# Rotary embedding on one core: the cosine and sine rows loaded into partitions 0 to 62 instead of 0 to 124

## The chip, the core and the metric

The kernel runs on one core of one Trainium2 chip. The metric is the time of one execution on the device in microseconds (us). A second source is a profiled execution, whose trace gives the start and end of every instruction, the landing of every DMA, and a record (start, duration, bytes) of every DMA packet. The "span" is the time in that trace from the first to the last instruction.

## The reference

`x` is 16 batches x 512 positions x 1024 columns of float32, that is 16 heads of 64. `cos` and `sin` are 512 x 32, one row for each position.

```
x1, x2 = x[..., :32], x[..., 32:]          # halves of each head
out = concatenate([x1 * cos - x2 * sin,
                   x1 * sin + x2 * cos], axis=-1)
```

33.6 MB of `x` go in, as much comes out, and each table is 64 KB.

## The kernel before

**Tiling.** `x` is cut into 8 slabs of 2 batches. Two slabs make a pair, and a pair lies in one SBUF tile of 128 partitions x 16,384 float32. Partition p of a pair holds 16 successive positions, 16(p mod 32) to 16(p mod 32)+15. The first 8 positions of every partition are the even slab, the other 8 the odd one. So the tables are needed in 32 different pieces of 16 positions (`TP` = 32), and each piece in four partitions: p, p+32, p+64, p+96. There are three places for pairs; the fourth pair (slabs 6 and 7) takes the first place again.

**The tables.** A piece is 16 positions x 32 numbers = 512 float32 = 2 KB. One DMA for each table (line 87) puts the 32 pieces into every fourth partition, 0, 4 ... 124 (`TS` = 4, line 35), of a tile that VectorE has cleared (line 86), so the other partitions hold zeros. VectorE casts both tables to bf16 (line 107). GpSimd builds the selection matrix `pick` (lines 97 and 100): for column j of each group of 32 columns it sets the row p with p - TS*j = 0 to 1 (and, in a second copy, to -1). TensorE multiplies (line 114): output partition p gets the table row of piece p mod 32, so every partition has its own cosines and sines, in two PSUM tiles, one for even and one for odd slabs. VectorE copies the first to a bf16 table `tab` (line 121), ScalarE the second (line 155).

**A slab's work.** ScalarE casts the float32 slab to bf16 in place (line 155); VectorE multiplies it by the two tables (line 171, two instructions) and adds the crossed halves (line 174); ScalarE casts back to float32 (line 155), and the pair is stored.

**Order of the DMAs.** All DMAs are issued by SyncE (line 66) in one queue, in program order: slab 0 (128 rows of 32 KB), the cosine table, the sine table, slab 1 (128 rows of 32 KB), then the two pairs of slabs 2 to 5, each as two DMAs of 64 rows of 64 KB (even partitions, odd partitions). Later come the stores of slabs 0-1, the loads of slabs 6-7 into the place that those stores leave, and the other three stores, each when ScalarE is done with its pair.

Of the kernel before, what the change touches and what calls it, by code (L numbers as in the profile page):

```python
# [2 lines left out]

# [4 lines left out]


@with_exitstack  # L10
def kernel(
    ctx: ExitStack,
    tc: tile.TileContext,
    x: bass.AP,
    cos: bass.AP,
    sin: bass.AP,
    num_heads: int,
    out: bass.AP,
):
    nc = tc.nc  # L20
    P = nc.NUM_PARTITIONS

    batch, seq, dim = x.shape
    nh = num_heads
    hd = dim // nh
    half = hd // 2
    bf16 = mybir.dt.bfloat16
    f32 = mybir.dt.float32

    nb = 2  # L30
    nslabs = batch // nb
    rpp = nb * seq // P
    W = rpp * dim
    TP = seq // (2 * rpp)
    TS = P // TP
    TW = 2 * rpp * half

    out_flat = out.rearrange("b s h d -> b s (h d)")

    singles = ctx.enter_context(tc.tile_pool(name="singles", bufs=1))  # L40
    pairs = ctx.enter_context(tc.tile_pool(name="pairs", bufs=3))
    psum = ctx.enter_context(tc.tile_pool(
        name="psum", bufs=1, space=bass.MemoryType.PSUM))


    def view(t, offset, *dims):
        return dataclasses.replace(t, offset=t.offset + offset,
                                   ap=[t.ap[0], *[list(d) for d in dims]])

    places = [pairs.tile([P, 2 * W], f32, tag="pair", name="pair") for _ in range(3)]


    def here(s, n=1):
        return view(places[s // 2 % 3], s % 2 * W, (1, n * W))


    def there(t, s, n=1):  # L60
        return bass.AP(tensor=t.tensor, offset=t.offset + s // 2 * 2 * P * W + s % 2 * W,
                       ap=[[2 * W, P], [1, n * W]])


    def issue(out, in_):
        tc.keep_in_program_order(nc.sync.dma_start(out=out, in_=in_))  # L66


    def load(s, n=1, parts=slice(None)):
        issue(here(s, n)[parts], there(x, s, n)[parts])  # L70


    def store(s, n=1, parts=slice(None)):
        issue(there(out_flat, s, n)[parts], here(s, n)[parts])


    EVEN, ODD = slice(0, P, 2), slice(1, P, 2)


    load(0)  # L80


    cos_sb = singles.tile([P, TW], f32, tag="cos_sb")
    sin_sb = singles.tile([P, TW], f32, tag="sin_sb")
    for t, src in ((cos_sb, cos), (sin_sb, sin)):
        nc.vector.memset(t, 0.0)  # L86
        issue(t[::TS], bass.AP(
            tensor=src.tensor, offset=src.offset, ap=[[TW, TP], [1, TW]]))

    load(1)  # L90
    for s in (2, 4):
        for parts in (EVEN, ODD):
            load(s, 2, parts)


    pick = singles.tile([P, 2 * P], bf16, tag="pick")
    nc.gpsimd.memset(pick, 0.0)  # L97
    for g in range(2):
        part = view(pick, g * P, (TP, P // TP), (1, TP))
        nc.gpsimd.affine_select(  # L100
            out=part, in_=part, compare_op=mybir.AluOpType.not_equal,
            fill=1.0 - 2.0 * g, base=0, pattern=[[0, P // TP], [-TS, TP]],
            channel_multiplier=1)

    tab1 = singles.tile([P, 2 * TW], bf16, tag="tab1")
    for i, t in enumerate((cos_sb, sin_sb)):
        nc.vector.tensor_copy(out=view(tab1, i * TW, (1, TW)), in_=t)  # L107

    accs, tabs = [], []
    for h in range(2):  # L110
        acc = psum.tile([P, 2 * rpp * hd], f32, tag=f"acc{h}", name="acc")
        for i in range(2):
            for f in range(2):
                nc.tensor.matmul(  # L114
                    view(acc, i * rpp * hd + f * half, (hd, rpp), (1, half)),
                    view(pick, i * f * P, (1, P)),
                    view(tab1, i * TW + h * rpp * half, (half, rpp), (1, half)),
                    start=True, stop=True)
        accs.append(acc)
        tabs.append(singles.tile([P, 2 * rpp * hd], bf16, tag=f"tab{h}", name="tab"))  # L120
    nc.vector.tensor_copy(out=tabs[0], in_=accs[0])  # L121

    PART = 3 * dim
    LAST = {1: dim, 3: dim // 2}
    passes = []
    for s in range(nslabs):
        r = 0  # L130
        for n in {0: (4, 4), nslabs - 1: (4, 2, 2)}.get(s, (rpp,)):
            passes.append((s, r, n))
            r += n


    def halves(u):
        s, r, n = u
        t = here(s).bitcast(bf16)
        return [view(t, (2 * r + i * n) * dim, (1, n * dim)) for i in range(2)]


    def cast(u, a=0, b=None):
        s, r, n = u
        m = (n * dim if b is None else b) - a
        copy(view(halves(u)[0], a, (1, m)), view(here(s), r * dim + a, (1, m)))


    def copy_out(u, a=0, b=None):
        s, r, n = u
        m = (n * dim if b is None else b) - a  # L150
        copy(view(here(s), r * dim + a, (1, m)), view(halves(u)[1], a, (1, m)))


    def copy(out, in_):
        tc.keep_in_program_order(nc.scalar.copy(out=out, in_=in_))  # L155


    for i, u in enumerate(passes):
        s, r, n = u
        if i == 0:  # L160
            cast(u)
            cast(passes[1])
            copy(tabs[1], accs[1])
            cast(passes[2])
        elif s > 0 and not r:
            for v in passes:
                if v[0] == s + 1:
                    cast(v, PART if v[0] == 3 else 0)
        lo, up = halves(u)
        for t, a in ((up, 0), (lo, rpp * hd)):  # L170
            nc.vector.tensor_mul(  # L171
                out=t, in0=lo,
                in1=view(tabs[s % 2], a + r * hd, (hd, n), (0, nh), (1, hd)))
        nc.vector.tensor_add(  # L174
            out=up, in0=up, in1=view(lo, half, (hd, n * nh), (-half, 2), (1, half)))

        if s == 1:
            copy_out(u, 0, n * dim - LAST[s])
            cast((3, 0, rpp), 0, PART)
            copy_out(u, n * dim - LAST[s])  # L180
            for act in (store, load):
                for parts in (EVEN, ODD):
                    act(0 if act is store else 6, 2, parts)
        elif s == 3:
            copy_out(u, 0, n * dim - LAST[s])
        else:
            copy_out(u)
        if s == 4:
            copy_out((3, 0, rpp), rpp * dim - LAST[3])
            store(2, 2)  # L190
        elif s > 4 and s % 2 and r + n == rpp:
            for parts in (EVEN, ODD) if s == 5 else (slice(None),):
                store(s - 1, 2, parts)


# [1 line left out]
_INS = ['x', 'cos', 'sin', 'num_heads']  # L197
_OUTS = [((16, 512, 16, 64), 'float32')]

_NUMBERS = {'num_heads': 16}  # L200


# [26 lines left out]
```

## Time and profile before

| | |
|---|---|
| time, median of 3 runs (lowest to highest) | 161.15 us (160.95 to 161.81) |
| time of the profiled execution | 161.17 us |
| its span | 159.4 us (1.77 us lie around it) |
| ScalarE (ACT) busy | 114.3 us, 72% of the span |
| VectorE (DVE) busy | 109.6 us, 69% |
| TensorE (PE) busy | 1.9 us in 8 matmuls |
| DMA | 67.24 MB, mean 422 GB/s over the span |
| granted TensorE clock | 1.0 |

How to read it: the busy shares are of the whole span. The DMA packets' time is given as a share of 16 DMA engines' span: at 100% all sixteen would move data from the first instruction to the last. "SPq" is the queue of SyncE, from which every DMA here is issued; a DMA's line shows the issue, and its landing is a time of its own. Where a line ends in "<-", the name behind the arrow is what ended the wait.

### The profile page before, as it was taken

The numbers are of one execution on the slowest core, as the hardware profiler recorded it, in microseconds if no ns is written. First come the engines' busy times: TensorE is split into PE (matmuls) and PEld (weight loads), VectorE is DVE, ScalarE is ACT, GpSimd is POOL, SyncE is SP. The second block draws the span as 40 slices with busy tenths as digits, with TensorE's granted clock in tenths as the row PEclk, the third lists the DMA queues.
The fourth block names the chain that finished last, engine by engine and source line by source line (L and its number), as shares of the span: only waits on it lengthen the run. The fifth ranks groups of instructions, "written<-read, shape, count | busy, mean of one in ns | idle before, by whom it ended". The sixth has DMA issues, their size and how long they took to land.

```text
span 159.4 us, 178 instructions
## 1 busy us (share of the span) xinstructions
PE 1.9 (1%) x8; PEld 1.1 (1%) x8; DVE 109.6 (69%) x38; ACT 114.3 (72%) x27; POOL 1.1 (1%) x7
## 2 busy tenths in 40 slices
PE   0004000000000000000000000000000000000000
PEld 0002000000000000000000000000000000000000
DVE  2004899999806998999899999909999997000000
ACT  3007949992399999999999996799999969400000
POOL 2000000000000000000000000000000000000000
DMA  7999999899799699699698996996996996996993
GB/s 263 395 395 444 493 411 526 378 411 526 313 477 526 280 510 526 263 526 526 263 526 362 428 526 263 526 526 263 526 510 280 526 510 280 526 493 296 526 395 132
DMA packets 1472, 67.24 MB, mean 422 GB/s; under 512 B 256, under 2 KB 256, under 8 KB 320
## 3 DMA queue, kind: packets, MB, share of 16 engines
q1 hardware_dynamic: 1472, 67.24, 98.0%
HBM read 33.69 MB, written 33.55 MB: 422 GB/s over the span
## 4 chain that ended last, share of the span: by engine, by line
DMA 50%; DVE 15%; ACT 13%; issue 6%; ACTq 2%; SPq 1%
DMA pair<-in_x_dram 36%; DMA out_dram<-pair 14%; ACT pair L155 13%; DVE pair L171 10%; DVE pair L174 4%; ACTq L224 2%; SPq L66 1%; DVE sin_sb L86 0%; DVE cos_sb L86 0%; ACTq L155 0%
## 5 line engine op out<-in xcount | busy, mean ns | idle before, releaser
L155 ACT CAST pair<-pair 128x8192 bf16<-128x8192 f32 (+11 forms) x25 | 112.2, 4557 | 22.2 <-DMA pair<-in_x_dram 20.7
L171 DVE TENSOR_TENSOR pair<-pair,tab 128x8192 bf16<-128x8192 bf16 (+2 forms) x22 | 71.4, 3259 | 11.8 <-ACT pair L155 11.4
L174 DVE TENSOR_TENSOR pair<-pair 128x8192 bf16<-128x8192 bf16 (+2 forms) x11 | 35.8, 3259 | 0.3
L107 DVE CAST tab<-cos_sb 128x512 bf16<-128x512 f32 x1 | 0.4, 427 | 11.1 <-DMA cos_sb<-in_cos_dram 11.1
L114 PE MATMUL acc<-tab,pick 128*128 128x256 bf16 x8 | 1.9, 415 | 13.6 <-DVE tab L107 13.6
L121 DVE CAST tab<-acc 128x1024 bf16<-128x1024 f32 x1 | 1.2, 1225 | 1.0 <-PE acc L114 1.0
L155 ACT ACT_TABLE_LOAD x1 | 1.3, 1283 | 0.7 <-PEq L210 0.7
L114 PEld LDWEIGHTS <-pick 128*128 128x128 bf16 x8 | 1.1, 139 | 13.8 <-issue 12.0
L86 DVE MEMSET cos_sb<- 128x512 f32 x1 | 0.5, 485 | 0.9 <-PEq L210 0.9
L155 ACT CAST tab<-acc 128x1024 bf16<-128x1024 f32 x1 | 1.0, 1003 | 0.0
L100 POOL TENSOR_SCALAR_AFFINE_SELECT pick<-pick 128x128 bf16<-128x128 bf16 x2 | 0.6, 308 | 0.1
L86 DVE MEMSET sin_sb<- 128x512 f32 x1 | 0.5, 485 | 0.1
L107 DVE CAST tab<-sin_sb 128x512 bf16<-128x512 f32 x1 | 0.4, 421 | 0.0
L97 POOL MEMSET pick<- 128x256 bf16 x1 | 0.3, 311 | 0.3 <-POOLq L210 0.3
L210 POOL MEMSET const-bfloat16-1.0<- 128x1 bf16 x1 | 0.1, 101 | 0.0
L210 POOL MEMSET const-uint8-127<- 128x1 uint8 x1 | 0.1, 101 | 0.0
L210 POOL MEMSET const-float32-0.0<- 128x1 f32 x1 | 0.1, 98 | 0.2 <-issue 0.2
L210 POOL MEMSET const-float32-1.0<- 128x1 f32 x1 | 0.1, 98 | 0.0
## 6 DMA issues: line engine op xcount, KB each, us to landing
pair<-in_x_dram SPq DMA_DIRECT2D x2, 4096.0 KB, 16.1
pair<-in_x_dram SPq DMA_DIRECT2D x6, 33.8
out_dram<-pair SPq DMA_DIRECT2D x6, 21.5
cos_sb<-in_cos_dram SPq DMA_DIRECT2D x1, 64.0 KB, 11.6
sin_sb<-in_sin_dram SPq DMA_DIRECT2D x1, 64.0 KB, 11.1
```

Source lines behind the costliest of these rows:

```text
L66: tc.keep_in_program_order(nc.sync.dma_start(out=out, in_=in_))
L86: nc.vector.memset(t, 0.0)
L97: nc.gpsimd.memset(pick, 0.0)
L100: nc.gpsimd.affine_select(out=part, in_=part, compare_op=mybir.AluOpType.not_equal, fill=1.0 - 2.0 * g, base=0, pattern=[[0, P // TP], [-T ...
L107: nc.vector.tensor_copy(out=view(tab1, i * TW, (1, TW)), in_=t)
L114: nc.tensor.matmul(view(acc, i * rpp * hd + f * half, (hd, rpp), (1, half)), view(pick, i * f * P, (1, P)), view(tab1, i * TW + h * rpp * ...
L121: nc.vector.tensor_copy(out=tabs[0], in_=accs[0])
L155: tc.keep_in_program_order(nc.scalar.copy(out=out, in_=in_))
L171: nc.vector.tensor_mul(out=t, in0=lo, in1=view(tabs[s % 2], a + r * hd, (hd, n), (0, nh), (1, hd)))
L174: nc.vector.tensor_add(out=up, in0=up, in1=view(lo, half, (hd, n * nh), (-half, 2), (1, half)))
L210: nc = _bacc.Bacc("TRN2", target_bir_lowering=False, num_devices=1)
L224: with _tile.TileContext(nc) as tc:
```

## The change

The stride between the table pieces becomes 2 instead of 4, so the 32 pieces go to partitions 0, 2 ... 62. The slice of the destination gets an end, since partitions 64 to 126 are not written any more by these DMAs. The selection matrix follows through `TS` in the pattern of line 102 (row 2j instead of row 4j for column j). The instructions of every engine, their order, their sizes and their waits are the same in both kernels.

```diff
     TP = seq // (2 * rpp)
-    TS = P // TP
+    TS = P // TP // 2
     TW = 2 * rpp * half
...
     for t, src in ((cos_sb, cos), (sin_sb, sin)):
         nc.vector.memset(t, 0.0)
-        issue(t[::TS], bass.AP(
+        issue(t[:TP * TS:TS], bass.AP(
             tensor=src.tensor, offset=src.offset, ap=[[TW, TP], [1, TW]]))
```

## The prediction

> **What bounds the kernel now.** I read the engines' busy shares first, then the row of the DMA queue, then the slices of the span.
>
> ```profile
> PE 1.9 (1%) x8; PEld 1.1 (1%) x8; DVE 109.6 (69%) x38; ACT 114.3 (72%) x27; POOL 1.1 (1%) x7
> ...
> DMA  7999999899799699699698996996996996996993
> ...
> q1 hardware_dynamic: 1472, 67.24, 98.0%
> ```
>
> No compute engine is busy over 72%. The packets of the one DMA queue take 98.0% of sixteen engines' 159.4 us, that is 156.2 us on each engine. The digits of the slices swing between 6 and 9 because packets are long against a slice; the total says that no engine ever rests for long. The trace's packet records give the parts: 896 packets of 64 KB (2418 ns each for nearly all), 256 of 32 KB (1213 ns for most, the first sixteen up to 2045), and 64 of 2 KB, which are the two tables, 84 ns each without exception. The first packet starts at 1.73 us and the last ends at 158.23, a window of 156.5 us: about 0.3 us of it is unused on a mean engine. So the DMA engines are the bound from end to end, and whatever adds time to an engine's chain of packets comes out at the end of the kernel.
>
> Next I looked at who waits for the tables, in the timeline of the first stage and the waits.
>
> ```profile
> 12.81 7.11 ACT L155 CAST pair<-pair 128x4096 bf16<-128x4096 f32 x2 [10.81 <-DMA pair<-in_x_dram]
> 13.08 0.43 DVE L107 CAST tab<-cos_sb 128x512 bf16<-128x512 f32 x1 [11.14 <-DMA cos_sb<-in_cos_dram]
> 13.42 0.42 DVE L107 CAST tab<-sin_sb 128x512 bf16<-128x512 f32 x1
> 13.56 1.87 PE L114 MATMUL acc<-tab,pick 128*128 128x256 bf16 x8 [13.56 <-DVE tab L107]
> 13.56 1.38 PEld L114 LDWEIGHTS <-pick 128*128 128x128 bf16 x7 [11.99 <-issue]
> 14.82 1.23 DVE L121 CAST tab<-acc 128x1024 bf16<-128x1024 f32 x1 [0.98 <-PE acc L114]
> 16.45 6.82 DVE L171 TENSOR_TENSOR pair<-pair,tab 128x4096 bf16<-128x4096 bf16 x3 [0.41 <-ACT pair L155]
> ```
>
> ```profile
> ACT pair L155 <- DMA pair<-in_x_dram: 20.7, 4, 10.8
> ...
> DVE pair L171 <- ACT pair L155: 11.4, 5, 6.0
> ```
>
> The reader is to see that the tables land right behind slab 0 (the first cast starts at 12.81, the cosine cast at 13.08), and that the path from them (cast, matmul, copy to `tab`) ends at 14.82 + 1.23 = 16.05. VectorE's first multiply comes 0.4 us later, and what it waited for was ScalarE's cast. So the tables have 0.41 us to spare. Behind that lies more: ScalarE waits for a later load up to 42.25 us (5.38 us idle before it in the timeline), and VectorE waits for ScalarE for 6.0 us up to 49.30. A late table of up to 0.41 + 5.4 = 5.8 us is taken up before any store is late.
>
> **The change part by part.**
>
> Instructions: the order of each engine is the same in both kernels, with the same shapes and waits. VectorE's two clears (485 ns each) and two casts (427 and 421 ns) work on 128 partitions either way; GpSimd's two selections (308 ns) only take another step; the 8 matmuls (415 ns) still sum over 128 partitions, most of them zero. SyncE's two issues (567 and 577 ns) still have 32 rows of 2 KB. All this is 0 us, and it all lies before 16.45 us, beside loads that go on until 61 us.
>
> DMA: what is left is where the 64 packets of 2 KB go, in the stretch from 11.9 to 12.8 us. Today they are spread evenly: the sixteen completions of slab 0 come from 12.318 to 12.794 us, those of cosine from 12.524 to 12.982, those of sine from 12.709 to 13.155, each some 0.2 us behind the DMA ahead. That is two packets of 84 ns and a completion record of 9 ns, so each engine carries 2 + 2 table packets, 4 x 84 = 0.34 us of its 156.2.
>
> The trace has no DMA that writes only the lower 64 partitions: slabs 0 and 1 write all 128, and the loads by halves write every second partition from end to end. So the price is bounded from both sides. Lower end: the engines take rows by their number in the list, whatever the partition, and nothing is shared between engines on the way into SBUF: still 4 packets each, +0 us. Upper end by the even loads: the table work falls on half of the path, be it that an engine serves a fixed set of partitions (then 8 engines carry 8 packets each, 0.67 us, and 8 carry none), or that several engines meet at one entrance of SBUF (then 16 engines share 8 entrances, and each entrance passes twice the table bytes). Either way the slower half ends 8 x 84 - 4 x 84 = 336 ns later, **+0.34 us**. Below nothing: the sixteen engines do not end together (the last store's completions come from 157.97 to 158.56, 0.59 us apart). Were the eight that lose their table packets the late ones, the end could come up to 0.34 us sooner, -0.34 us.
>
> I take the upper end, +0.34. The rows nearest to it are the large packets. Sixteen engines move 64 KB each at the same time, and all but a few of 896 packets take the same 2418 ns, for DMAs of all partitions, of the even ones and of the odd ones, in and out. Were engines handed rows without regard to the partition, two of them would now and then meet at a place and one packet would be longer; such regularity fits a fixed share of the partitions for each engine. It fits a path without any sharing as well, which is the rival.
>
> [...]
>
> A delay of the tables by 0.34 us moves the end of the table path to 16.39, still ahead of 16.45, so VectorE does not wait. Slab 1 follows the tables in the queue and lands 0.34 us later on the slow engines, and from there every landing, every cast that waits for one, and the last store shift with it. The last store is issued at 137.28 while the DMA ahead of it lands from 138.66 on, so 1.38 us lie between; both ends shift alike, and no new gap opens.
>
> Sum against the profiled execution: 161.17 + 0.34 = 161.51 us. That execution is 0.02 above the median of 161.15, so no correction is made. A measurement of this kernel can tell about 0.5%, 0.8 us, from no change; the forecast is no difference that can be told.
>
> **The rivals.**
>
> The rows do not care about partitions: +0, 161.2 us. For it: 84 ns in every table packet, although they end beside 32 KB packets of other engines. Against it: the large packets' regularity. Chance 0.33.
>
> Balance: the engines that are relieved are the late ones, and the end comes 0.34 us sooner, 160.8 us. For it: a spread of 0.59 us at the end. Against it: the late ones would have to be all in one half of the engines. Chance 0.06.
>
> The other side, crowding on few engines: the 32 rows of step 2 go to so few engines that the tables clog their chains. All 64 packets are 64 x 84 = 5.38 us. On n engines the slowest chain grows by 5.38/n - 0.34. That exceeds 0.8 us only for n of 4 or less: 4 engines give +1.0, 162.2 us; 2 give +2.35, 163.5; one gives +5.0, 166.2. For it: the step and the span of the list are new to this kernel. Against it: DMAs of 128, 64 and 32 rows are all spread over sixteen completions now. A late table adds nothing even then, as 5.0 is under the 5.8 us of cover. Chance 0.10.
>
> That the change does not do what it says (engine and SBUF side unchanged) is the first rival.
>
> **How the numbers follow.** +0.34: 0.45; +0: 0.33; -0.34: 0.06; crowding: 0.10; a drift of the chip between the runs (the three runs of before lie 0.86 us apart) that moves a median by over 0.5%: 0.03 up and 0.03 down. Faster by over 0.5%: 0.03. Slower: 0.10 + 0.03 = 0.13. Within: 0.84. The range from 160.8 to 162.0 holds the first three cases (0.84) with 0.5 us for the runs' spread on top of the likeliest; crowding lies outside.
>
> **What would show it.** In the changed kernel's packet records the 64 table packets of 84 ns should be 8 on each of half the engines, or longer than 84 ns. The completions of the cosine DMA should trail those of slab 0 by 0.34 us on the slow engines instead of 0.2, and slab 1's last landing (22.82) should come at about 23.2. VectorE's first multiply stays at about 16.45 with a wait on ScalarE. The share of the DMA queue stays at 98%. If the sine cast starts over 1 us later than 13.42, the rows are crowded on few engines. If the time moves by over 0.8 us while the first 23 us of the trace stay as they are, my account is wrong at its root, for then something later in the kernel depends on these partitions.

## The result and the profile after

The changed kernel takes 163.26 us (median of 6 runs, 163.04 to 164.26) beside 161.28 us for the kernel before (6 runs): the ratio is 1.0134, 95% interval 1.0101 to 1.0167. It is slower by about 2 us, where the forecast was 0.34 us and no difference that can be told. The profiled execution took 163.04 us with a span of 161.2 us. (The ratios in this document leave disturbed runs out and are not the quotients of the medians.)

The first view is taken from the page of the changed kernel: busy shares, slices, and the DMA queue.

```profile
PE 1.9 (1%) x8; PEld 1.1 (1%) x8; DVE 109.7 (68%) x38; ACT 114.3 (71%) x27; POOL 1.1 (1%) x7
...
DMA  7999999979979979979799899899899899896990
...
q1 hardware_dynamic: 1472, 67.24, 97.5%
```

The compute engines do the same work in the same time. The DMA engines still move the same 67.24 MB in 1472 packets, and their packets take 97.5% of a longer span: 0.975 x 161.2 = 157.2 us on a mean engine, against 156.2 before. So the mean engine is busy for 1.0 us more with the same bytes, and idle for about 0.9 us more (the span grew by 1.86 us).

The next view is the timeline of the first stage after the change.

```profile
13.11 7.11 ACT L155 CAST pair<-pair 128x4096 bf16<-128x4096 f32 x2 [11.11 <-DMA pair<-in_x_dram]
13.54 0.43 DVE L107 CAST tab<-cos_sb 128x512 bf16<-128x512 f32 x1 [11.61 <-DMA cos_sb<-in_cos_dram]
13.90 0.43 DVE L107 CAST tab<-sin_sb 128x512 bf16<-128x512 f32 x1
...
15.29 1.23 DVE L121 CAST tab<-acc 128x1024 bf16<-128x1024 f32 x1 [0.96 <-PE acc L114]
16.75 6.82 DVE L171 TENSOR_TENSOR pair<-pair,tab 128x4096 bf16<-128x4096 bf16 x3 [0.24 <-ACT pair L155]
```

Slab 0 is cast 0.30 us later, the tables 0.46 us later, and the first multiply still waits for ScalarE's cast and not for the tables (15.29 + 1.23 = 16.52 is ahead of 16.75). The compute side takes the late tables without a wait, as forecast. Slab 0 was not to be late at all: its last completion comes at 13.09 us instead of 12.79, although its last packet ends at 12.43 us in both kernels, so the delay lies between the packets and their completions, in the time in which the table packets move.

The waits of the changed kernel:

```profile
ACT pair L155 <- DMA pair<-in_x_dram: 22.6, 4, 11.1
...
DVE pair L171 <- ACT pair L155: 12.6, 5, 6.1
```

ScalarE waits 1.9 us longer for the loads (20.7 before), which is all of the loss, and VectorE waits 1.2 us longer for ScalarE.

Where the time went is read from ScalarE's timeline, from the casts that wait for a landing. Each line starts when a load has landed on all engines. First the kernel before, then the changed one.

```profile
22.84 14.03 ACT L155 CAST pair<-pair 128x8192 bf16<-128x8192 f32 x3 [2.01 <-DMA pair<-in_x_dram]
42.25 55.89 ACT L155 CAST pair<-pair 128x8192 bf16<-128x8192 f32 x11 [5.38 <-DMA pair<-in_x_dram]
100.69 27.97 ACT L155 CAST pair<-pair 128x8192 bf16<-128x8192 f32 x6 [2.55 <-DMA pair<-in_x_dram]
```

```profile
23.34 14.03 ACT L155 CAST pair<-pair 128x8192 bf16<-128x8192 f32 x3 [2.21 <-DMA pair<-in_x_dram]
42.75 55.89 ACT L155 CAST pair<-pair 128x8192 bf16<-128x8192 f32 x11 [5.38 <-DMA pair<-in_x_dram]
102.54 27.96 ACT L155 CAST pair<-pair 128x8192 bf16<-128x8192 f32 x6 [3.90 <-DMA pair<-in_x_dram]
```

The loss comes in two parts. Slab 1 is 23.34 - 22.84 = 0.50 us late, and slabs 2-3 are as late as that (42.75 - 42.25): call this the **front part**. The next cast that waits, for slabs 6-7, is 102.54 - 100.69 = 1.85 us late: 1.35 us were lost between 42 and 101 us, the **late part**. Behind it nothing is lost: the last store's last completion comes 57.88 us after that cast starts, and 57.87 us in the kernel before.

The packet records say where between 42 and 101 us. The last load of slabs 4-5 lands completely at 62.02 us (61.52 before: still 0.50 late), the second store at 81.57 (81.23), the even half of slabs 6-7 at 92.80 (90.90). So it happens where the queue goes from stores to loads. I add up, over all 16 engines, by how much the packets of 64 KB that start from 75 to 85 us are longer than 2418 ns: it is 4.55 us in the kernel before and 13.58 us in the changed one. The packets that grow are mainly the last one of each engine in the store (they start at about 78 us) and the first ones of the load (about 81 us). It falls unevenly: the sixteen completions of the even load lie between 90.32 and 90.90 us before, and between 91.06 and 92.80 after. The slowest engine decides, since the cast waits for all sixteen (the completions of the odd half of slabs 6-7 lie between 100.73 and 102.46 us in the changed kernel, and the cast starts at 102.54). The last store then waits for the casts, and the faster engines wait for it: it is issued at 139.12 us, engines that were done from 139.05 us on start its first packets at 139.97, and so they stand idle for up to 0.9 us. In the kernel before they go on without a rest.

### The profile page after: what moved, and what is told of

It reads as the page before. It is cut to its first block, busy times and chain, and to the rows that moved or that the text cites. A ratio compares the mean times of both kernels' runs of the same rounds, so it can differ in the third digit from the quotient of the medians.

```text
span 161.2 us, 178 instructions
## 1 busy us (share of the span) xinstructions
PE 1.9 (1%) x8; PEld 1.1 (1%) x8; DVE 109.7 (68%) x38; ACT 114.3 (71%) x27; POOL 1.1 (1%) x7
## 2 busy tenths in 40 slices
DMA packets 1472, 67.24 MB, mean 417 GB/s; under 512 B 256, under 2 KB 256, under 8 KB 320
## 3 DMA queue, kind: packets, MB, share of 16 engines
q1 hardware_dynamic: 1472, 67.24, 97.5%
## 4 chain that ended last, share of the span: by engine, by line
DMA 50%; DVE 14%; ACT 13%; issue 6%; ACTq 2%; SPq 1%
DMA pair<-in_x_dram 37%; DMA out_dram<-pair 13%; ACT pair L155 13%; DVE pair L171 10%; DVE pair L174 4%; ACTq L224 1%; SPq L66 1%; DVE sin_sb L86 0%; DVE cos_sb L86 0%; ACTq L155 0%
## 5 line engine op out<-in xcount | busy, mean ns | idle before, releaser
L171 DVE TENSOR_TENSOR pair<-pair,tab 128x8192 bf16<-128x8192 bf16 (+2 forms) x22 | 71.4, 3258 | 13.1 <-ACT pair L155 12.6
```

The costliest lines, as they stand in the source:

```text
L171: nc.vector.tensor_mul(out=t, in0=lo, in1=view(tabs[s % 2], a + r * hd, (hd, n), (0, nh), (1, hd)))
```

## Experiments

**Probe: what a list of partitions costs.** DMAs alone, without any arithmetic; the output is not the rotation.

```diff
+    FOUR, LOW, HIGH, ONE = (slice(0, P, 4), slice(0, P // 2, 2),
+                            slice(P // 2, P, 2), slice(0, P // 4))
...
+    rows(big[0], slice(None), 0, P, W)
+    for k, parts in enumerate((FOUR, LOW, ONE)):
+        dst = view(small, k * 8 * TW, (TW, 8), (1, TW))
+        issue(dst[parts], bass.AP(tensor=x.tensor, offset=x.offset + k * 8 * TP * TW,
                                  ap=[[TW, TP], [TP * TW, 8], [1, TW]]))
+        rows(big[k + 1], slice(None), (k + 1) * P, P, W)
+    for k, parts in enumerate((FOUR, LOW, HIGH, ONE)):
+        rows(big[k], parts, 512 + k * TP, TP, W)
```

> DMAs alone, all arithmetic left out, and the output is not the rotation. Four loads of 128 rows of 32 KB; between them 32 rows of 8 x 2 KB to every fourth partition, then to partitions 0, 2 ... 62, then to partitions 0 to 31. Then 32 rows of 32 KB each to every fourth partition, to 0, 2 ... 62, to 64, 66 ... 126, and to 0 to 31. If engines meet at 8 entrances: 2 KB rows on every fourth partition cost 16 x 84 ns = 1.34 us, on the other two sets 2.7 us; large rows on every fourth partition 1213 ns a packet, on the other three sets 2426 ns. If 8 engines take all the rows: the same total, but with 1213 ns a packet and four packets on each of 8 engines. If the partition does not matter: 1.34 us and 1213 ns throughout.

The diff shows only the lines that set the partitions; `rows` loads n rows of 32 KB, and `big` and `small` are places in SBUF.

The view is a table by stretches; the last two columns are the DMA share and GB/s. The stretches are 32 rows of 32 KB to every fourth partition, to 0 ... 62, to 64 ... 126, to 0 ... 31, and then a store of 128 rows.

```profile
48.80:51.20 2.40, 0.00 (x0) 1.00 1.36 423
51.30:56.00 4.70, 0.00 (x0) 1.00 0.96 202
56.10:61.00 4.90, 0.00 (x0) 1.00 1.01 214
61.10:65.80 4.70, 0.00 (x0) 1.00 0.82 202
66.80:75.40 8.60, 0.00 (x0) 1.00 1.00 431
```

Each of the three lists that stay in one half of the partitions runs at half the rate (202, 214 and 202 GB/s instead of 423), be it every second partition of the half or 32 in a row. The engines stay busy all the while (share 0.82 to 1.01), their packets only last longer: the 64 that start from 55.2 us on take 2247 to 2571 ns instead of 1213. So the engines together get half the rate on one half of the partitions, as in the prediction's case of engines that meet on the way into SBUF, and the rival by which eight engines take all the rows is out. At what they meet, and how many such entrances there are, was not shown.

The 2 KB rows repeat the disputed cost four times over, 16 packets on each engine where this kernel has 4. On every fourth partition all packets take 84 ns and the whole DMA 1.32 us (first completion to first completion of the load ahead). On 0 ... 62 most take about 160 ns and the DMA 2.47 us, and the load behind them needs 10.10 us instead of 9.77. That is 1.15 + 0.33 = 1.48 us for 16 packets an engine, so by proportion an estimate of 0.37 us for 4.

**The changed kernel again, and the upper half.** The first is the changed kernel without any edit; the second has this one on top of it:

```diff
-        issue(t[:TP * TS:TS], bass.AP(
+        issue(t[P // 2::TS], bass.AP(
...
-            fill=1.0 - 2.0 * g, base=0, pattern=[[0, P // TP], [-TS, TP]],
+            fill=1.0 - 2.0 * g, base=-(P // 2), pattern=[[0, P // TP], [-TS, TP]],
```

> The changed kernel once more, as a control. In its first profile the end is 1.86 us later than before: slab 1's last landing is 0.50 us later, and that stays so until the last load of slabs 4-5 lands at 62.0 us; the first load of slabs 6-7 (even partitions) lands another 1.4 us later. Theory A (the change causes both, by way of the order in which the engines run after the tables): ratio 1.013 again, with 0.4 to 0.5 us at slab 1 and 1 to 2 us more at the first load of slabs 6-7. Theory B (the late part is chance, a matter of one profile): the times would be 0.3 to 0.5 us above before, and the late part would be gone or another size.

> The 32 pieces go to partitions 64, 66 ... 126 instead of 0, 2 ... 62. Theory A with shared entrances (half of the partitions have half of the entrances): slab 1's last landing 0.3 to 0.5 us later than before, as in the changed kernel, and a total of about 163 us. Rival (the low partitions themselves, or the first eight engines, are what is slow): slab 1 lands as before, at 22.8 us, and the total is 161.2 us.

ScalarE's casts of slabs 2-3 and 6-7, the changed kernel again and then with the tables in the upper half:

```profile
42.80 55.89 ACT L155 CAST pair<-pair 128x8192 bf16<-128x8192 f32 x11 [5.37 <-DMA pair<-in_x_dram]
102.45 27.97 ACT L155 CAST pair<-pair 128x8192 bf16<-128x8192 f32 x6 [3.76 <-DMA pair<-in_x_dram]
```

```profile
42.84 55.89 ACT L155 CAST pair<-pair 128x8192 bf16<-128x8192 f32 x11 [5.37 <-DMA pair<-in_x_dram]
102.71 27.97 ACT L155 CAST pair<-pair 128x8192 bf16<-128x8192 f32 x6 [3.98 <-DMA pair<-in_x_dram]
```

Again: 163.14 us beside 161.40, ratio 1.0082 (1.0048 to 1.0116); front part 0.55 us (casts at 42.80), late part 1.21 us (102.45). Upper half: 163.14 us, ratio 1.0098 (1.0067 to 1.0130), front 0.59, late 1.43. Both parts come back, so theory B (chance of one profile) falls, and no half is the slower one. Single executions of the changed kernel go from 162.15 to 164.26 us. Those of the kernel before are scattered too: 4 of the 25 beside these runs took 162.15 to 162.93 us. No trace of such an execution was kept, so it is not shown that the kernel before has a late part in them.

**Twice: a delay without crowding.** On top of the kernel before, each table is loaded again on every fourth partition of a tile that nobody reads.

```diff
+    for k, src in enumerate((cos, sin)):
+        again = singles.tile([P, TW], f32, tag=f"again{k}", name="again")
+        issue(again[::TS], bass.AP(
+            tensor=src.tensor, offset=src.offset, ap=[[TW, TP], [1, TW]]))
+
     load(1)
```

> The kernel before with two more table loads of 64 KB each behind the first two, every fourth partition, into tiles that nobody reads. It adds 4 packets of 84 ns to every engine, evenly: all landings from slab 1 on should be 0.34 us later. Theory A1 (any delay of 0.3 to 0.5 us at the front moves the meeting of stores and loads at 75 to 83 us and brings the late 1.4 us): about 163 us. Theory A2 (only an uneven disturbance of the engines brings it): 161.6 us.

161.53 us, ratio 1.0001 (0.9976 to 1.0025). ScalarE's timeline:

```profile
42.64 55.89 ACT L160 CAST pair<-pair 128x8192 bf16<-128x8192 f32 x11 [5.37 <-DMA pair<-in_x_dram]
100.84 27.96 ACT L160 CAST pair<-pair 128x8192 bf16<-128x8192 f32 x6 [2.31 <-DMA pair<-in_x_dram]
```

The front is 0.39 us late and 0.24 us of it is won back by 101 us. A delay of nearly the same size, spread evenly, has no late part, though four table DMAs stand in the queue instead of two. A1 falls.

**The extra loads crowded, at four places.** The same loop as in the last diff, on top of the kernel before, but into `again[:P // 2:2]` (partitions 0 to 62). The real tables stay where they were; only the place in the queue differs: behind the tables (moving at 13 us), behind slabs 2-3 (42 us), behind slabs 4-5 and ahead of the first store (61 us), behind slabs 6-7 and ahead of the third store (100 us).

> The kernel before (tables in every fourth partition), with both tables loaded once more into partitions 0, 2 ... 62 of tiles that nobody reads, in the queue behind the last load of slabs 4-5, so that they move at about 61 us. Theory A2 (crowding on half the entrances leaves the engines out of step, and the next change from stores to loads, at 75 to 83 us, pays for that): 0.5 us more from 61 us on and 1 to 1.5 us more at the first load of slabs 6-7, about 163.2 us. Rival C (the late part belongs to the real tables or to the first 20 us): 0.5 us only, 161.8 us.

> The same two extra loads into partitions 0, 2 ... 62, but behind the last load of slabs 6-7, so that they move at about 100 us, after the only change from stores to loads. Theory A2: 0.3 to 0.5 us, 161.8 us, with the first load of slabs 6-7 as in the kernel before (last landing 90.9 us). Rival (crowding costs the same wherever it stands): 163 us.

> The kernel before with two extra table loads into partitions 0, 2 ... 62 of tiles that nobody reads, right behind the real ones, which stay in every fourth partition. Since the same two loads at 61 us brought no late part, theory D says that crowding has to stand among loads, where it changes the order of the engines for good: 0.34 + 0.5 us at slab 1, and 1 to 1.5 us more at the first load of slabs 6-7, about 163.3 us. Rival E (the late part belongs to where the real tables lie and what reads them): 0.8 us and no more, 162.0 us.

> The same two extra loads between slabs 2-3 and slabs 4-5, so that they move at about 42 us, with loads ahead of and behind them. Theory D: 0.5 us from 42 us on and 1 to 1.5 us more at the first load of slabs 6-7, about 163 us. Rival E, or a rival by which only the first 20 us count: 0.5 us, 161.8 us.

| extra loads at | median us | ratio (95%) |
|---|---|---|
| 61 us | 161.74 | 1.0037 (1.0006 to 1.0067) |
| 100 us | 162.06 | 1.0040 (1.0014 to 1.0065) |
| 13 us | 163.31 | 1.0118 (1.0072 to 1.0165) |
| 42 us | 163.14 | 1.0121 (1.0067 to 1.0175) |

The casts of slabs 6-7 with the extra loads at 61 us, then with those at 42 us, then with those at 13 us:

```profile
101.21 27.97 ACT L160 CAST pair<-pair 128x8192 bf16<-128x8192 f32 x6 [2.96 <-DMA pair<-in_x_dram]
```

```profile
102.19 27.97 ACT L160 CAST pair<-pair 128x8192 bf16<-128x8192 f32 x6 [3.71 <-DMA pair<-in_x_dram]
```

```profile
102.64 27.97 ACT L160 CAST pair<-pair 128x8192 bf16<-128x8192 f32 x6 [3.35 <-DMA pair<-in_x_dram]
```

At 61 us they cost 0.52 us (101.21 - 100.69) and bring no late part, so theory A2 in its first form, by which any crowding ahead of the change from stores to loads would do, fell here. At 100 us they cost 0.57 us at the end of the last store, as A2 had it. For the other two places I had then formed theory D: crowding has to stand among loads. The times came out so (163.31 and 163.14 us, forecast 163.3 and 163), the parts did not: the delay by the landing of slabs 4-5 was larger than forecast and the late part smaller, so the sums agree partly by luck. At 42 us the casts of slabs 6-7 are 1.50 us late, and 0.86 us of that was there when slabs 4-5 had landed. At 13 us it is 1.95 us, of which 1.15 came by then. Late parts of 0.64 and 0.80 us are left, and since the real tables are not touched, they are not theirs.

The place is not the same as in the changed kernel either. Of these late parts, 0.45 and 0.51 us arise in the odd half of slabs 6-7, in last packets that start at about 99 us, where the queue goes from loads to the third store; one of them takes 2932 ns at 42 us and one 3009 ns at 13 us. With the loads at 42 us all packets from 75 to 85 us together grow by 1.66 us, less than the 4.55 us of the kernel before, and the mean of the sixteen completions of the last load is 0.80 us late, no more than at slabs 4-5 (0.93). So there a few packets on the slowest engine make the late part, and not a dearer meeting as a whole.

**A rest of the queue behind slab 1.** In both kernels a copy that reads slab 1 makes SyncE wait for the landing of slab 1 (it issues the copy at 23.07 us in the kernel before and at 23.41 in the changed one), and all engines start again together.

```diff
     load(1)
+    rest = singles.tile([P, TW], f32, tag="rest")
+    issue(rest, view(places[0], W, (1, TW)))
```

> The kernel before with a rest of the queue behind slab 1: a copy of 2 KB a partition from slab 1 to a tile that nobody reads is issued next, so SyncE waits until slab 1 has landed (22.8 us) before it issues more, and all engines run dry and start again together. It is the partner of the next run. Expected: about 2 to 3 us more than before, 163.5 to 164.5 us, with an excess over the usual packet time in the first packets after the rest.

> The changed kernel with the same rest behind slab 1. Theory A2 (what the tables leave behind is the order in which the engines run, and a common start wipes it out): no more than 0.5 us above the kernel before with the rest, and the first load of slabs 6-7 as there. Rival (something else of the change acts late): 1.9 us above it, as without the rest.

Kernel before with the rest: 166.37 us, ratio 1.0306 (1.0236 to 1.0376). Changed kernel with the rest: 167.82 us, ratio 1.0371 (1.0287 to 1.0456). The kernel before with the rest was expected at 163.5 to 164.5 us. The medians are 1.45 us apart, nearer to the rival's 1.9 than to the 0.5 of theory A2, and the intervals overlap, so the times leave the pair open. The two profiles, before and changed, lie closer, but that of the kernel before shows the longest of its four executions (167.32 us, the others 166.05 to 166.52):

```profile
46.19 55.89 ACT L157 CAST pair<-pair 128x8192 bf16<-128x8192 f32 x11 [6.68 <-DMA pair<-in_x_dram]
106.73 27.97 ACT L157 CAST pair<-pair 128x8192 bf16<-128x8192 f32 x6 [4.65 <-DMA pair<-in_x_dram]
```

```profile
46.53 55.89 ACT L157 CAST pair<-pair 128x8192 bf16<-128x8192 f32 x11 [6.66 <-DMA pair<-in_x_dram]
107.29 27.97 ACT L157 CAST pair<-pair 128x8192 bf16<-128x8192 f32 x6 [4.87 <-DMA pair<-in_x_dram]
```

The casts of slabs 2-3 are 0.34 us apart and those of slabs 6-7 0.56 us. What I had not expected is that the kernel before now has a late part, with tables on every fourth partition: 106.73 - 46.19 = 60.54 us between those casts against 58.44 without the rest, 2.10 us more. In that execution, then, a late part came without any crowded list. Its usual size is not known, as the other three executions were 0.8 to 1.3 us shorter, and this pair does not show that a common start wipes out what the tables leave behind.

**No meeting of stores and loads.** In both kernels the odd half of slabs 6-7 is loaded first; it waits for the second store, so the queue is dry in between (the two loads are issued from 80.93 us on in the kernel before, from 71.25 without the exchange).

```diff
-                for parts in (EVEN, ODD):
+                for parts in (EVEN, ODD) if act is store else (ODD, EVEN):
```

> The kernel before with the odd half of slabs 6-7 loaded ahead of the even half. The first of the two loads then waits for the second store to land, and the queue runs dry between stores and loads. Partner of the next run. Expected 2 to 3 us above before (a landing, an issue and a start without work on the queue): 163.5 to 164.5 us.

> The changed kernel with the same exchange. If the late part is the price of the meeting of the last store packets with the first load packets, it cannot arise where the queue is dry between them: 0.5 us above its partner and no more. If it is something else that the changed tables do around 80 us, 1.9 us above its partner.

165.07 us, ratio 1.0238 (1.0213 to 1.0263), and 165.81 us, ratio 1.0289 (1.0253 to 1.0325). The difference is 0.74 us, no longer 2, if more than the 0.5 us expected; the kernel before was expected at 163.5 to 164.5 us. ScalarE's timelines, before and changed:

```profile
42.33 55.89 ACT L155 CAST pair<-pair 128x8192 bf16<-128x8192 f32 x11 [5.37 <-DMA pair<-in_x_dram]
104.52 27.97 ACT L155 CAST pair<-pair 128x8192 bf16<-128x8192 f32 x6 [6.30 <-DMA pair<-in_x_dram]
```

```profile
42.83 55.89 ACT L155 CAST pair<-pair 128x8192 bf16<-128x8192 f32 x11 [5.38 <-DMA pair<-in_x_dram]
105.13 27.96 ACT L155 CAST pair<-pair 128x8192 bf16<-128x8192 f32 x6 [6.41 <-DMA pair<-in_x_dram]
```

The front part stays (0.50 us at 42 us) and hardly any late part is left (0.61 us at 105 us). The exchange costs 3.9 us in the kernel before (165.07 beside 161.20), so it is no remedy. In its profile 2.6 us of that are there when the first load of slabs 6-7 has landed (93.52 us, 90.90 before), and 1.2 us more come with the second, whose last packets, ahead of the third store, take 3184 to 3819 ns. The pair agrees with the place that the packet records give for the changed kernel, the last store packets and the first load packets. It does not settle it alone: a dry queue also makes all engines start anew, which could even out what the tables leave behind, wherever that acts.

**Equal halves.** The first run adds, on top of the changed kernel, the loop of the extra loads into `again[P // 2::2]`, so that the upper half is crowded as much as the lower. The second splits each table over both halves, 16 rows in either, which is as many as every fourth partition puts there; its selection matrix is built in two parts to match, which the diff leaves out:

```diff
-        issue(t[:TP * TS:TS], bass.AP(
-            tensor=src.tensor, offset=src.offset, ap=[[TW, TP], [1, TW]]))
+        for k in range(2):
+            issue(t[k * P // 2:k * P // 2 + TP:TS], bass.AP(
+                tensor=src.tensor, offset=src.offset + k * TP // 2 * TW,
+                ap=[[TW, TP // 2], [1, TW]]))
```

> The changed kernel, with both tables loaded once more into partitions 64, 66 ... 126 of tiles that nobody reads, right behind the real ones. If the late part comes from the inequality of the two halves, it goes: about 0.9 us more at slab 1 and nothing later, 162.2 us, below the changed kernel although it moves more. If any crowding leaves the bad order, the late 1.2 to 1.5 us stay: 163.6 us.

> Each table as two DMAs of 16 rows: pieces 0 to 15 into partitions 0, 2 ... 30 and pieces 16 to 31 into 64, 66 ... 94, with the selection matrix to match. [...] If the bytes at each entrance set the price and the order, 161.3 to 161.6 us, like before. If the stride of 2 is what hurts, or 16 engines on 8 entrances for one row each are enough to bring the bad order, 162.5 to 163.3 us.

Both halves crowded: 163.64 us, ratio 1.0138 (1.0108 to 1.0168), as expected if any crowding leaves the bad order. Its casts come at 43.22 and 102.27: a front part of 0.97 us and a late part of 0.61 in the profiled execution, which at 162.96 us is one of the shorter of its six (162.63 to 164.21). Two lists: 162.92 us, ratio 1.0100 (1.0063 to 1.0137), with casts at 42.73 and 102.13: the front part is 0.48 us and the late part 0.96, although each half of the partitions gets as many bytes as before. So inequality of the halves, summed over both DMAs, is not what is needed. That one DMA's rows stay in one half of the partitions while they move is what these versions have in common; the expectation named the stride of 2 beside it, and no run here takes the two apart for the late part (for the rate the probe does: 32 partitions in a row are as slow as a stride of 2, 202 GB/s beside 202 and 214).

## Why the prediction was wrong, point by point

**The bound and the compute side: right in the main.** DMA is the bound, every engine does the same work in the same time, and VectorE's first multiply still waits for ScalarE, at 16.75 us and not at 16.45, because slab 0 lands 0.30 us later. That "whatever adds time to an engine's chain of packets comes out at the end of the kernel" is too simple in both directions: in the run twice 0.39 us at slabs 2-3 was 0.18 us at the last completion, and in the changed kernel 0.50 us became 1.86.

**The front term: right in kind, too small.** I took +0.34 us, the upper end, for either of two mechanisms, a fixed set of partitions for each engine or engines that meet at an entrance. That the table work falls on half of the path was my assumption; no row of the kernel before shows it, and no run shows how many entrances there are. The probe showed half the rate (202 to 214 GB/s instead of 423) and packets of 2247 to 2571 ns instead of 1213, which fits the second mechanism, and its 2 KB rows give an estimate of 0.37 us. My reason for the upper end, that the regular large packets fit a fixed share of the partitions for each engine, speaks for the first one, which the probe rules out for lists like this; so that the upper end was the better choice is partly luck. The profiles show 0.50 to 0.59 us at slab 1 for the slowest engine, and 0.38 us for the mean of its sixteen completions (22.60 to 22.98). I had also expected packets over 84 ns. Only 3 of 64 were longer; the crowding shows in the next packet of each engine, 32 KB of slab 1, which takes 1439 to 1675 ns, most about 1510, instead of 1213. Whoever looks at the small packets alone sees nothing.

**The step that failed** is this one: "from there every landing, every cast that waits for one, and the last store shift with it ... and no new gap opens". It treats a delay as something that is only carried along, and so puts every loss behind slab 1 at nothing. The runs showed a second loss in its place, of 1.2 to 1.4 us on the slowest engine in three profiles, and in the changed kernel its place: the last packets of the second store and the first ones of the next load, where the packets' excess goes from 4.55 to 13.58 us over 16 engines. From 20 to 60 us the loads carry the delay on with hardly any loss (their excess is under 0.3 us per 5 us, over all engines). A new gap did open too: the 1.38 us between the last store's issue and the first landing ahead of it shrank to 0.25 us, and the faster engines stood idle for up to 0.9 us. What it is that the tables leave behind, and that acts 60 us later, stays open; another order in time of the sixteen engines is argued below. The kernel before pays at that place too; its two packets of over 3000 ns were in the records, and the prediction passed over them with "all but a few".

**The rivals.** "The rows do not care" was wrong by the probe (423 GB/s on every fourth partition, 202 to 214 in one half). "Balance" was wrong in sign. "Crowding on few engines" got the side right, but not the mechanism: all sixteen engines took part. My own test line, that a move of over 0.8 us with an unchanged front would mean that something later depends on these partitions, came half true: the front moved, but by 0.5 us only, and something later in the kernel did depend on what the table loads had done (two extra loads that nobody reads were enough).

**What stays open.** Shown are the place of the late part in the changed kernel (the packet records, with which the dry pair agrees), that an even delay does not bring it (twice), and that crowded extra loads bring one when they stand among loads (13 and 42 us) and not ahead of stores (61 us) or behind the last load (100 us). With the loads at 13 and 42 us more than half of it came at another place, ahead of the third store. That the carrier is the order of the engines in time is argued, not shown: the loads run on with the same spacing from 23 to 62 us (the sixteen completions of a load lie 0.58 us apart at both ends in the changed kernel, 0.46 us in the kernel before), so a difference made at 13 us is still there later, and nothing else was seen to last. The packet records do not name the engine, so which engines have to follow each other closely for the meeting to be dear was not seen. The spread alone does not tell good from bad: at the last load of slabs 4-5 it is 0.42 us in the second profile of the changed kernel and 0.30 with the extra loads at 42 us, both with a late part, and 0.70 with those at 61 us, without one. No version here beats the kernel before.

## What to carry to other kernels

Each DMA to SBUF should have its rows in both halves of the partitions even when it is small (161.28 us with the tables in both, 163.26 in one); two lists with one half each did not help here (two lists: 162.92 us). A list that stayed in one half ran at half the rate in the probe (202 to 214 GB/s instead of 423), and in the kernel the price shows in the packet behind it (about 1510 ns instead of 1213). Where the DMA engines are the bound, do not cost a disturbance as a delay alone: look where stores and loads follow each other in the queue, compare the last completion of a DMA there with the mean of its sixteen, and count the slowest engine. In this kernel the packets that were longer than their neighbours in the profile before (up to 3067 ns instead of 2418, at 77.5 us) marked the place that became dearer.

## What the runs showed of the hardware that was not expected

With 4 crowded 2 KB packets an engine, 61 of 64 keep their 84 ns, and the next 32 KB packet takes 0.3 us more. In the kernel before and the changed one, packets of 64 KB take 2418 ns with hardly a loss from 20 to 75 us; where stores give way to loads, the excess over all engines is 4.55 us in the one and 13.58 in the other. The total alone does not give the time: it is 1.66 us there with the extra loads at 42 us, which are slower than the kernel before, since the slowest engine decides. A common start of all engines costs 9 to 13 us over all engines in the first 64 KB packets: 12.6 us in the kernel before with a rest and 8.9 in the changed one with it, 12.7 and 11.9 at the start of the loads in the dry pair.
